# Where layer 1's first-norm modulation is computed: in layer 0's mixer, or at the end of layer 0's routing

## The chip, the cores and the metric

The kernel runs on one core of a Trainium2 chip. The metric is the device time of one execution, in microseconds (us), as the median over several executions. Within a core, PE is TensorE (matmuls; PEld its weight loads), DVE VectorE, ACT ScalarE, POOL GpSimd and SP SyncE, whose queue issues most DMAs here. Each engine works through its own instructions in order and waits on semaphores for the others.

## The reference

Two layers; each has an adaLN-modulated mixer and an adaLN-modulated mixture of experts. Cut to what bears on the change (c and c_ctx are vectors of 1024; x and ctx have 256 tokens each):

```python
for l in range(DEPTH):                                   # DEPTH = 2
    mod  = silu(c) @ w_mod[l] + b_mod[l]                 # 1024 x 6144
    sh1, sc1, g1, sh2, sc2, g2 = split(mod, 6)
    modc = silu(c_ctx) @ w_mod[l] + b_mod[l]             # the same for the context
    h_l = rmsnorm(xl, norm1_g[l]) * (1 + sc1) + sh1
    h_c = rmsnorm(xc, norm1_g[l]) * (1 + sc1c) + sh1c
    o_l, o_c = mixer(h_l, h_c, ...)                      # attention + SSD, w_out
    xl, xc = xl + g1 * o_l, xc + g1c * o_c
    y = hier_moe(h2 of all tokens, ...)                  # 4 groups x 8 experts, top 2
    xl, xc = xl + g2 * y_l, xc + g2c * y_c
return rmsnorm(xl, final_g)
```

The change concerns `sh1, sc1` and their context twins of layer 1. They depend on `c`, `c_ctx` and weights alone, so they can be computed at any time before layer 1's mixer.

## The kernel before

The kernel goes through layer 0's mixer (0 to some 258 us), its routing (output projection, second norm, router, to some 342 us), a branch for token counts over an expert's capacity, layer 0's experts (352 to some 615 us), and then the same for layer 1.

The two products `sh1, sc1` of layer 1 are 1024 x 2048 weights, cut into eight blocks of 1 MB. `mod_norm1(l)` (L203 ff.) is a generator that handles one block at a time: load the block into a tile of the pool `wh` ("wl"), eight matmuls that leave 32 x 256 partial sums each in four column groups (L221; a float32 matmul counts twice in the trace, so a block is 16 instructions there), a copy of the sums from PSUM to SBUF on DVE (`mr`, L223), two small matmuls that add the four groups and turn the result over (L227, four instructions in the trace), and three small DVE operations that make one column of `b1` (shift) and `a1` (norm gain times 1 + scale) of them (L228 to L230). A list `MODS` puts the modulations of a layer into one chain, and a planner weaves that chain with attention and SSD by estimated costs. In before, `MODS[0]` has three entries, and the third, `(1, 0)`, is `mod_norm1(1)`: its eight blocks lie between 213 and 259 us, near the end of layer 0's attention.

Layer 0's routing ends in a stretch that is ordered by hand. After the last router matmuls (`rmat`, L1110), `pick` finds the experts of the tokens on DVE, with one matmul group (L1161); `place` gives each token its slot in an expert's list (PE L1168, L1169), `onehot` and `spread` (PE L1195) write these lists, a GpSimd gather then fetches the token rows, `count` (PE L1463, DVE L1465, L1466) makes the largest count of an expert, `cmi`. Every engine loads `cmi` and takes or passes over the branch of `fallback` (L1805). The branch's body is only run when an expert has more tokens than its capacity. Behind it stand the last three loads of layer 0's first experts (`LATE`), the turning of the gathered rows (L1584, then `xgT`, L1593 and L1595), and the first expert matmul (L1608).

The tiles of the first experts' weights come from a ring ("R"), the pool `big` ("B", ten tiles of 1 MB) and the pool `wh` ("W"), in the order of the string `LOAD_TAGS[0]`; some come in quarters into small tiles (L256). Their DMAs are issued by SP, in order. `big` is the only pool of the three that the change also uses.

Of the kernel before, what the change touches and what calls it, by code (L numbers as in the profile page):

```python
# [4 lines left out]
F32 = mybir.dt.float32  # L5
# [15 lines left out]
BIG_BUFS = 10  # L21
LOOK = 3
BIG = 1.0e30
LOAD_TAGS = ("RBBBBBBBBWWWWBB", "RBBBBBBWWWWBBBB")
RAW = ("RRRBRRR", "RBBRRRR")
H2M = "AVAV"
H2A = "GGGGVVVV"
# [28 lines left out]
TAIL_ENG = {ET.PE, ET.DVE, ET.Activation, ET.Pool}  # L56
FIN_ENG = {ET.PE, ET.DVE, ET.Activation, ET.Pool}
ME = {ET.PE}
MODS = (((0, 1), (0, 2), (1, 0)), ((1, 1), (1, 2)))
ATT_W = (70.0, 45.0)  # L60
SSD_W = (28.0, 15.0)
MOD_W = (28.0, 18.0)
# [18 lines left out]
def _tile_kernel(tc, A, out, dbg=None):  # L81
# [15 lines left out]
    def bk():  # L97
        return psB.tile([128, 512], F32, tag="bk", name="bk")
# [13 lines left out]
    def big(name, dt=F32):  # L112
        return P.tile([128, 2048], dt, tag="big", name=name, bufs=BIG_BUFS)
# [13 lines left out]
    def sm(shape, tag, bufs=1, dt=F32):  # L127
        return P.tile(shape, dt, tag=tag, name=tag, bufs=bufs)
# [46 lines left out]
    def kcs(n):  # L175
        o, w = KC[n]
        return kd[:, o - KC_A:o - KC_A + w] if o >= KC_A else kc[:, o:o + w]

    def cps(n, l):
        o, w = CPK[n]  # L180
        return cpk[:, o + l * (w // 2):o + (l + 1) * (w // 2)]
# [30 lines left out]
    def mod_norm1(l, pre=()):  # L212
        a1 = cp.tile([128, 2, 8], F32, tag="a1", name="a1", bufs=2)
        b1 = cp.tile([128, 2, 8], F32, tag="b1", name="b1", bufs=2)
        modT[l, "a1"], modT[l, "b1"] = a1, b1
        for b in range(8):
            w = pre[b] if b < len(pre) else rload(A["wm0"][l, b], [128, 8, 256], big("wm") if pre else None)
            pm = md_()
            for k in range(8):
                g = k % 4  # L220
                T.matmul(pm[32 * g:32 * g + 32, 0:256], csT[:, k, :], w[:, k], start=(k < 4), stop=(k >= 4))  # L221
            mr = tw("bm", 2, "mr")[:, 0:256]
            V.tensor_copy(mr, pm[:, 0:256])  # L223
            yield 0.9
            pt = tp()
            for s in range(2):
                T.matmul(pt[:, 2 * s:2 * s + 2], mr[:, s * 128:(s + 1) * 128], kcs("sel"), start=True, stop=True)  # L227
            V.tensor_scalar(b1[:, :, b], pt[:, 0:2], cps("bsh", l)[:, b:b + 1], None, op0=ALU.add)  # L228
            V.tensor_scalar(a1[:, :, b], pt[:, 2:4], cps("bsc", l)[:, b:b + 1], 1.0, op0=ALU.add, op1=ALU.add)
            V.tensor_scalar(a1[:, :, b], a1[:, :, b], cps("n1g", l)[:, b:b + 1], None, op0=ALU.mult)  # L230
            yield 0.1

    def qload(src, tags, after=None):
        q = []
# [760 lines left out]
    def route_out(l, oT):  # L995
# [12 lines left out]
        for hf in range(2):  # L1008
            for b in range(2):
                wo[b, hf] = rload(A["wout"][l, b, hf], [128, 4, 512], big("wo") if WOB[l][2 * hf + b] == "B" else wh("wo"))  # L1010
        R = {}
        R["lg"] = sm([128, 4, 36], "lg")
        R["m1"] = sm([128, 4, 1], "m1")
        R["v8"] = sm([128, 4, 8], "v8")
# [148 lines left out]
        def place(pair):  # L1163
            s2 = slice(pair[0], pair[0] + 2)
            M, pk = Mf[:, s2], pkf[:, s2]
            j = pair[0] - qt[0]
            pp = pos[:, 32 * j:32 * j + 64]
            T.matmul(pp, lt, M, start=(j == 0), stop=False)  # L1168
            T.matmul(pp[:, 32:64], ones, M[:, 0], start=False, stop=True)  # L1169
            for t in pair:  # L1170
                for k in range(2):
                    V.scalar_tensor_tensor(tk2[:, t, k], keyf[:, t], k8[:, t, k:k + 1], pp[:, 32 * (t - pair[0]):32 * (t - pair[0]) + 32],
                                           op0=ALU.is_equal, op1=ALU.mult)
            V.reduce_sum(pk, tk2[:, s2], axis=AX.X)
            if l:
                sd = sm([128, 2, 2], "sd")
                ob = sm([128, 2, 2], "ob")
                er = sm([128, 2, 2], "er")
                V.scalar_tensor_tensor(er, k8[:, s2, 0:2], 1.0, k8[:, s2, 0:2], op0=ALU.is_ge, op1=ALU.subtract)
                V.scalar_tensor_tensor(sd, er, 64.0 * cap, pk, op0=ALU.mult, op1=ALU.add)  # L1180
                V.tensor_scalar(ob, pk, float(cap), 1.0e6, op0=ALU.is_ge, op1=ALU.mult)
                V.tensor_tensor(sd, sd, ob, op=ALU.add)
                for i in range(2):
                    V.tensor_tensor(R["sid"][:, i], sd[:, i].unsqueeze(2).to_broadcast([128, 2, 8]),
                                    boff.unsqueeze(1).to_broadcast([128, 2, 8]), op=ALU.add)
                return
            for t in pair:
                onehot(t)
            spread(pair)
# [40 lines left out]
        def h2w(t):  # L1230
            (nc.sync if t < 2 else nc.scalar).dma_start(h2d[l][t * 128:(t + 1) * 128, :], hres[t])
            dump(f"h2_{l}_{t}", hres[t])
# [74 lines left out]
        with tc.manual_schedule(engines=TAIL_ENG):  # L1307
            for b in range(2):
                prod(7, 2, b, tail)
                mul(2, b, banks[b, 2])  # L1310
            add(2, 0, G)
            add(2, 1, G)
            if l == 0:
                h2p(2, 0)
            prod(6, 3, 0, held)
            prod(7, 3, 0, tail)
            mul(3, 0, banks[0, 3], ("p", 3))
            add(3, 0, V)
            prod(6, 3, 1, held)
            prod(7, 3, 1, tail)  # L1320
            mul(3, 1, banks[1, 3], ("p", 3))
            add(3, 1, V)
            turn(2, 0)
            turn(3, 0)
            sqr(2, 0)
            mean(2, 0, 0)
            keep(2, 0, S)
            sqr(3, 0)
            mean(3, 0, 0)
            turn(2, 1)  # L1330
            rmat(2, 0)
            turn(3, 1)
            keep(3, 0, V)
            rmat(3, 0)
            sqr(3, 1)
            mean(3, 1, 1)
            root(3)
            keep(2, 1, V)
            rmat(2, 1)
            sqr(2, 1)  # L1340
            mean(2, 1, 1)
            root(2)
            if l == 0:
                h2p(2, 1)
            keep(3, 1, V)
            rmat(3, 1)
            if l == 0:
                h2s(2, 0)
                h2s(2, 1)
                h2a(3, 0, V)  # L1350
                h2b(3, 0, G)
                h2a(3, 1, V)
                h2b(3, 1, G)
                h2w(3)
            pick(prev)
            if l == 0:
                h2b(2, 0, G if HB[0] == "G" else V)
                h2b(2, 1, G if HB[1] == "G" else V)
                h2w(2)
                for t in prev:  # L1360
                    tokens(t)
            place(prev)
# [27 lines left out]
    def moe(l, R):  # L1390
# [121 lines left out]
        if l == 0:  # L1512
            count()
            R["gates"]()
            S.activation(sm([128, 1], "warm"), mhalf[:, 0:1], AF.Silu)
            fallback(l, R, gt4, cmi)
            for i in LATE[l]:
                load(i, gate)
# [441 lines left out]
```

## Time and profile before

| | |
|---|---|
| median of 3 runs | 1053.13 us (1052.07 to 1054.06) |
| the profiled execution | 1051.03 us, span 1049.2 us |
| mean granted TensorE clock | 0.964 |
| busy share of the span | PE 89%, DVE 59%, POOL 34%, ACT 32% |
| moved by DMA | 306 MB, mean 292 GB/s |

The profiled execution is 2.1 us under the median of the runs, and its span 1.8 us under its own time. Times of the rows are microseconds from the span's start. A busy share is an average over stages: in layer 0's attention PE is busy nearly all the time, in layer 0's routing it is not, in layer 1's experts the DMA is.

### The profile page before, as it was taken

To read this page: it belongs to the slowest core of one execution; us is meant where nothing else is said; L and a number is where in the kernel's file an instruction comes from. 1 tells how busy PE (TensorE), PEld (TensorE's weight loads), DVE (VectorE), ACT (ScalarE), POOL (GpSimd) and SP (SyncE) were. 2 spreads that over 40 slices of the span, in tenths; PEclk is the share of its full clock that TensorE was granted. 3 is DMA by queue.
4 is the path that set the end of the run, shared out by engine and by line. 5 is a ranking of instruction groups with operands and counts; after the bars stand their busy time and mean duration, and the time that the engine had idled before them with its cause. 6 is when DMAs were issued, how large, how long until landed. Compare 5 with 4: busy or idle time off the path is not lost. (4 is left out here: it accounts for less than half of the span.)

```text
span 1049.2 us, 14473 instructions
## 1 busy us (share of the span) xinstructions
PE 937.4 (89%) x5244; PEld 547.5 (52%) x5244; DVE 621.3 (59%) x1351; ACT 333.8 (32%) x689; POOL 356.2 (34%) x366
## 2 busy tenths in 40 slices
PE   5999999999987699999999979999999798786776
PEld 3778745566766344444444428683678543332232
DVE  4587079886688246666666667847886543222123
ACT  4465344544452110111112136543464211110102
POOL 2130035320175247667676560003331021111013
PEclk9999999999997799999999999999999898989989
DMA  9612377786748879899999835647486899998994
GB/s 375 208 43 79 141 302 248 281 309 221 294 126 295 288 306 404 335 418 419 419 419 420 341 111 171 239 163 261 173 315 248 281 417 419 419 419 353 421 414 159
DMA packets 54674, 306.20 MB, mean 292 GB/s; under 512 B 6168, under 2 KB 7064, under 8 KB 22976
## 3 DMA queue, kind: packets, MB, share of 16 engines
q1 hardware_dynamic: 49120, 288.10, 70.1%
q0 software_dynamic: 4224, 15.21, 4.6%
q10 hardware_dynamic: 1248, 1.86, 0.5%
q8 instruction: 44, 0.72, 0.3%
q14 instruction: 38, 0.31, 0.1%
HBM read 300.89 MB, written 4.26 MB: 291 GB/s over the span
## 5 line engine op out<-in xcount | busy, mean ns | idle before, releaser
L1673 POOL TENSOR_TENSOR xs<-xs,tmp 128x512 f32<-128x512 f32 x144 | 180.3, 1289 | 182.8 <-DVE tmp L1672 178.2
L1608 PE MATMUL bk<-we,xgT 128*64 128x512 f32 (+1 forms) x926 | 189.1, 615 | 14.6 <-DMA we<-wgu 14.6
L1643 PE MATMUL sc<-we,sa 128*64 128x512 f32 (+1 forms) x448 | 107.1, 645 | 17.5 <-DMA we<-wdn 17.5
L1608 PEld LDWEIGHTS bk<-we,xgT 128*64 128x64 f32 (+1 forms) x926 | 53.9, 126 | 124.0 <-issue 93.1
L1613 ACT ACTIVATE sa<-bk 128x256 f32<-128x256 f32 x24 | 9.2, 383 | 258.1 <-PE bk L1608 258.1
L1658 DVE SCALAR_TENSOR_TENSOR yl<-sc,gs,yh 128x512 fp32r<-128x512 f32 x46 | 34.4, 747 | 72.3 <-ACT yh L1657 72.3
L1643 PEld LDWEIGHTS sc<-we,sa 128*64 128x64 f32 (+1 forms) x448 | 28.2, 132 | 77.4 <-issue 43.5
L1657 ACT ACTIVATE yh<-sc,gs 128x512 fp32r<-128x512 f32 x46 | 31.6, 687 | 104.5 <-PE sc L1643 100.4
L1614 DVE TENSOR_TENSOR sa<-sa,bk 128x256 f32<-128x256 f32 x24 | 9.9, 412 | 71.6 <-ACT sa L1613 71.6
L770 PE MATMUL sc<-kT,qT 128*128 128x512 f32 (+1 forms) x96 | 45.7, 559 | 0.0
L792 PE MATMUL py<-pT,vt 128*64 128x128 f32 x320 | 43.6, 280 | 1.1 <-DVE oT L821 1.1
L1608 PE MATMUL bk<-ring,xgT 128*64 128x512 f32 (+1 forms) x80 | 40.5, 651 | 3.6 <-issue 2.5
L1072 DVE TENSOR_TENSOR lo<-wo,hi 128x512 fp32r<-128x512 f32 x44 | 33.8, 772 | 16.2 <-PE sc L1255 8.6
L1649 DVE TENSOR_SCALAR P<-kc,tid 128x128 fp32r<-128x128 f32 x80 | 40.8, 567 | 1.1 <-PE bk L1608 0.6
L792 PEld LDWEIGHTS py<-pT,vt 128*64 128x64 f32 x320 | 32.5, 136 | 15.4 <-issue 8.2
L774 ACT ACTIVATE p<-sc,mx 128x512 f32<-128x512 f32 (+1 forms) x48 | 29.4, 612 | 33.7 <-DVE mx L772 26.6
L401 PE MATMUL bk<-wh,hH 128*128 128x256 f32 (+1 forms) x128 | 39.8, 311 | 0.2
L1672 DVE TENSOR_TENSOR tmp<-bk,g 128x512 f32<-128x512 f32 x37 | 25.6, 691 | 23.9 <-POOL xs L1673 23.6
L403 PE MATMUL bk<-wh,hL 128*128 128x256 f32 (+1 forms) x128 | 38.0, 297 | 1.1 <-DVE hL L382 1.0
L785 ACT ACTIVATE pT<-tp 128x512 f32<-128x512 f32 (+1 forms) x48 | 24.9, 522 | 41.2 <-PE tp L783 41.1
L1582 PE MATMUL tp<-PT,h 128*128 128x128 f32 x256 | 34.3, 298 | 4.1 <-DVEq L1805 2.1
L1582 PEld LDWEIGHTS tp<-PT,h 128*128 128x128 f32 x256 | 32.8, 211 | 9.6 <-issue 5.4
(426 smaller groups left out, 2161.8 us busy)
## 6 DMA issues: line engine op xcount, KB each, us to landing
we<-wgu SPq DMA_DIRECT2D x109, 1024.0 KB, 17.7
we<-wdn SPq DMA_DIRECT2D x55, 1024.0 KB, 15.8
wl<-wmod SPq DMA_DIRECT2D x22, 1024.0 KB, 5.0
wl<-wm SPq DMA_DIRECT2D x10, 1024.0 KB, 8.1
ring<-wgu SPq DMA_DIRECT2D x10, 1024.0 KB, 19.8
wo<-wout SPq DMA_DIRECT2D x8, 1024.0 KB, 5.8
we<-wgu SPq DMA_DIRECT2D x27, 256.0 KB, 5.1
wm<-wm SPq DMA_DIRECT2D x6, 1024.0 KB, 12.2
```

Of the source, the lines that this page charges most:

```text
L401: T.matmul(o, a[0], b[0], start=start, stop=False)
L403: T.matmul(o, a[1], b[0], start=False, stop=stop)
L770: T.matmul(pm[:, 0:nk], qT[:, e, t * 128:(t + 1) * 128], kT[:, e, 0:nk], start=True, stop=True)
L792: T.matmul(py[e * 64:(e + 1) * 64, 0:128], vts[0][:, k, h * 64:(h + 1) * 64], pT[:, k * 128:(k + 1) * 128], start=(k == 0), stop=(k == nk ...
L1072: eng.tensor_tensor(lo, src, hi.bitcast(F32), op=ALU.subtract)
L1582: T.matmul(p_, R["hres"][t][:, c], xg[j], start=(j == 0), stop=(j == nT - 1))
L1608: T.matmul(pg[c], xgT[b][part][:, k, c], w[i][k], start=(part == 0 and k == 0), stop=(part == 1 and k == 3))
L1643: T.matmul(pd[h][c], aT[:, k, c], w[i][2 * k + h], start=(k == 0), stop=(k == 1))
L1649: V.tensor_scalar(Pm[b][:, j * 128:(j + 1) * 128], iota, tid[:, j, b:b + 1], None, op0=ALU.is_equal)
L1657: S.activation(yh, pd[h], AF.Copy, scale=gs[:, b:b + 1])
L1658: V.scalar_tensor_tensor(yl, pd[h], gs[:, b:b + 1], yh.bitcast(F32), op0=ALU.mult, op1=ALU.subtract)
L1673: (eng or (V if EADD[l][n] == "V" or alt and n % 2 else G)).tensor_tensor(xs[:, t, hs_], xs[:, t, hs_], tmp, op=ALU.add)
```

## The change

`(1, 0)` leaves `MODS[0]`, so `mod_norm1(1)` is no longer woven with layer 0's attention. A new generator `mod_next(1)` does its work in the routing. It has four tiles of the pool `big` ("wm"); blocks 0 to 3 are fetched by SP at once, blocks 4 to 7 each into the tile of the block four before it, once that block's matmuls are issued. `rows(b)` is the eight matmuls (now L253) and a copy of the sums to SBUF on ACT (L257) in place of DVE. The two small matmuls (L266) write into the same PSUM bank (`bk`, two buffers) as the sums, and two ACT operations (L267, L268) in place of three on DVE make the columns of `b1` and `a1`; a term `off` for the latter is made once on POOL. The matmuls of a block come ahead of the small ones of the block before it.

The generator is stepped by hand: its fetches at the start of the routing, three steps ahead of `pick(prev)` (blocks 0 to 3), one in `place` for the last pair of token tiles (block 4), and the rest after `count()` and ahead of the branch. In `LOAD_TAGS[0]` the four "W" move four places ahead, and a setting halves the memory in which GpSimd's DMA descriptors are kept.

```diff
-LOAD_TAGS = ("RBBBBBBBBWWWWBB", "RBBBBBBWWWWBBBB")
+LOAD_TAGS = ("RBBBBWWWWBBBBBB", "RBBBBBBWWWWBBBB")
-MODS = (((0, 1), (0, 2), (1, 0)), ((1, 1), (1, 2)))
+MODS = (((0, 1), (0, 2)), ((1, 1), (1, 2)))
+    def mod_next(l):
+        a1 = cp.tile([128, 2, 8], F32, tag="a1", name="a1", bufs=2)
+        b1 = cp.tile([128, 2, 8], F32, tag="b1", name="b1", bufs=2)
+        modT[l, "a1"], modT[l, "b1"] = a1, b1
+        off = sm([128, 8], "off")
+        G.tensor_scalar(off, cps("bsc", l), 1.0, None, op0=ALU.add)
+        G.tensor_tensor(off, off, cps("n1g", l), op=ALU.mult)
+        tiles = [big("wm") for _ in range(4)]
+
+        def fetch(b):
+            nc.sync.dma_start(tiles[b % 4], A["wm0"][l, b])
+
+        for b in range(4):
+            fetch(b)
+        yield
+        def rows(b):
+            w = tiles[b % 4].rearrange("p (k c) -> p k c", k=8)
+            pm = bk()
+            for k in range(8):
+                g = k % 4
+                T.matmul(pm[32 * g:32 * g + 32, 0:256], csT[:, k, :], w[:, k], start=(k < 4), stop=(k >= 4))
+            if b < 4:
+                fetch(b + 4)
+            mr = sm([128, 256], "mr", 2)
+            S.activation(mr, pm[:, 0:256], AF.Copy)
+            return pm, mr
+
+        cur = rows(0)
+        for b in range(8):
+            pm, mr = cur
+            if b < 7:
+                cur = rows(b + 1)
+            for s in range(2):
+                T.matmul(pm[:, 256 + 2 * s:258 + 2 * s], mr[:, s * 128:(s + 1) * 128], kcs("sel"), start=True, stop=True)
+            S.activation(b1[:, :, b], pm[:, 256:258], AF.Identity, bias=cps("bsh", l)[:, b:b + 1])
+            S.activation(a1[:, :, b], pm[:, 258:260], AF.Identity, bias=off[:, b:b + 1], scale=cps("n1g", l)[:, b:b + 1])
+            yield
@@ start of the routing
-        R = {}
+        nxt = mod_next(1) if l == 0 else iter(())
+        take(nxt, 1)
+        R = {"next": nxt}
@@ place
+            if pair[0] == 2:
+                take(nxt, 1)
             for t in pair:
                 onehot(t)
             spread(pair)
@@ the end of the routing
                 h2w(3)
+            take(nxt, 3)
             pick(prev)
@@ ahead of the branch
             count()
             R["gates"]()
+            drain(R["next"])
             S.activation(sm([128, 1], "warm"), mhalf[:, 0:1], AF.Silu)
             fallback(l, R, gt4, cmi)
@@
-    nc = bacc.Bacc("TRN2", target_bir_lowering=False, num_devices=1)
+    nc = bacc.Bacc("TRN2", target_bir_lowering=False, num_devices=1, dynamic_dma_scratch_size=8192)
```

Lines above the new function keep their numbers; below it a line of before stands 38 to 44 lines further down in the changed kernel.

On PE, in layer 0's attention, this stands in before (L770 scores, L783 turning of the probabilities, L792 values, L753 and L760 projections, L221 and L227 the modulation):

```order
L221 MATMUL md<-wl,kc 32x256 x8
L770 MATMUL sc<-kT,qT 128x512
L783 MATMUL tp<-kc,p 128x128 x4
L792 MATMUL py<-pT,vt 64x128 x4
L753 MATMUL bk<-kvqa,wl 128x512
L760 MATMUL bk<-kvqa,wl 128x512 x2
L227 MATMUL tp<-kc,mr 128x2 x2
L221 MATMUL md<-wl,kc 32x256 x5
L760 MATMUL bk<-kvqa,wl 128x512 x2
L221 MATMUL md<-wl,kc 32x256 x3
```

and this in the changed kernel (the same steps are L808, L821, L830, L791 and L798; L1078 is a small product for the router):

```order
L808 MATMUL sc<-kT,qT 128x512
L821 MATMUL tp<-kc,p 128x128 x4
L830 MATMUL py<-pT,vt 64x128 x2
L798 MATMUL bk<-kvqa,wl 128x512 x2
L1078 MATMUL md<-ke,sh_1490 128x36 x4
L798 MATMUL bk<-kvqa,wl 128x512 x2
```

The blocks are gone from between the attention's steps, and nothing has taken their place.

On PE, from the end of the router to the branch, before has `pick` (L1161), `place` (L1168, L1169), `spread` (L1195), `count` (L1463) and the branch:

```order
L1161 MATMUL md<-ke 128x64 x2
L1168 MATMUL md<-ke,kd 128x64
L1169 MATMUL md<-ke 128x32
L1195 MATMUL md<-rv,oh 128x32 x4
L1463 MATMUL md<-ke 128x32 x4
L1804 TENSOR_LOAD cmi
L1805 COMPARE_AND_BRANCH
```

The changed kernel has there first the blocks 0 to 3 and then the same steps with block 4 among them (L1201 is `pick`, L1208 and L1209 `place`, L1237 `spread`):

```order
L253 MATMUL bk<-wm,kc 32x256 x16
L266 MATMUL bk<-kc,mr 128x2 x2
L253 MATMUL bk<-wm,kc 32x256 x8
L266 MATMUL bk<-kc,mr 128x2 x2
L253 MATMUL bk<-wm,kc 32x256 x8
L266 MATMUL bk<-kc,mr 128x2 x2
L1201 MATMUL md<-ke 128x64 x2
L1208 MATMUL md<-ke,kd 128x64
L1209 MATMUL md<-ke 128x32
L253 MATMUL bk<-wm,kc 32x256 x8
L266 MATMUL bk<-kc,mr 128x2 x2
L1237 MATMUL md<-rv,oh 128x32 x4
```

and behind them `count` (L1506) and the blocks 5 to 7, up to the branch:

```order
L266 MATMUL bk<-kc,mr 128x2 x2
L253 MATMUL bk<-wm,kc 32x256
L1506 MATMUL md<-ke 128x32 x4
L253 MATMUL bk<-wm,kc 32x256 x7
L266 MATMUL bk<-kc,mr 128x2 x2
L253 MATMUL bk<-wm,kc 32x256 x8
L266 MATMUL bk<-kc,mr 128x2 x2
L253 MATMUL bk<-wm,kc 32x256 x8
L266 MATMUL bk<-kc,mr 128x2 x2
L1848 TENSOR_LOAD cmi
L1849 COMPARE_AND_BRANCH
```

All eight blocks now stand ahead of the branch, five of them ahead of `spread` and three between `count` and the branch.

On ACT, in the same stretch, before has two DMA issues and the two exponentials of the gates, and then the branch. The changed kernel has these, with the copies (L257) and the columns (L267, L268) around them (L1417 is the exponential that was L1374):

```order
L1273 DMA h2d_2251<-h_2911 128x1024
L257 ACTIVATE mr<-bk 128x256 x2
L267 ACTIVATE b_2261<-bk,kd 128x2
L268 ACTIVATE a_2260<-bk,off,kd 128x2
L1416 ACTIVATE e_3037<-e_3037 128x16
L1417 ACTIVATE gt<-dv 128x4
L257 ACTIVATE mr<-bk 128x256
L267 ACTIVATE b_2261<-bk,kd 128x2
L268 ACTIVATE a_2260<-bk,off,kd 128x2
L257 ACTIVATE mr<-bk 128x256
L267 ACTIVATE b_2261<-bk,kd 128x2
L268 ACTIVATE a_2260<-bk,off,kd 128x2
```

The copy of block 2 and all behind it now stand behind L1417, which waits for DVE's `dv`.

## Rows read from the trace of the kernel before

**Rows 1.** The page's part 1, busy time and share of the span:

```profile
PE 937.4 (89%) x5244; PEld 547.5 (52%) x5244; DVE 621.3 (59%) x1351; ACT 333.8 (32%) x689; POOL 356.2 (34%) x366
```

**Rows 2.** Windows; columns: length, busy PE, PEld, DVE, ACT, POOL, clock, DMA share, GB/s:

```profile
200.00:225.00 25.00, 25.00 (x163) 14.29 (x165) 21.17 (x55) 10.52 (x28) 7.42 (x9) 1.00 0.80 296
225.00:250.00 25.00, 24.58 (x198) 16.87 (x186) 19.32 (x59) 11.91 (x34) 7.60 (x8) 1.00 0.78 292
```

**Rows 3.** Lines by form, 125 to 300 us: the modulation's matmuls:

```profile
L221 PE MATMUL md<-wl,kc 128*32 128x256 f32 x128 | 10.6, 387 | 0.0
```

**Rows 4.** PE's timeline around one block in the weave (start, duration, line):

```profile
213.38 1.07 PE L221 MATMUL md<-wl,kc 128*32 128x256 f32 x16
214.38 1.12 PE L770 MATMUL sc<-kT,qT 128*128 128x512 f32 x2
...
219.13 0.50 PE L227 MATMUL tp<-kc,mr 128*128 128x2 f32 x4
219.57 1.05 PE L221 MATMUL md<-wl,kc 128*32 128x256 f32 x10
```

**Rows 5.** PE's timeline at the kernel's start, where layer 0's own blocks stand:

```profile
11.70 1.94 PE L221 MATMUL md<-wl,kc 128*32 128x256 f32 x16 [11.70 <-DVE xn L425]
13.57 1.12 PE L435 MATMUL py<-kc,xn 128*128 128x128 f32 x4
14.48 0.85 PE L227 MATMUL tp<-kc,mr 128*128 128x2 f32 x4
15.19 1.09 PE L435 MATMUL tp<-kc,xn 128*128 128x128 f32 x4
...
24.44 0.48 PE L402 MATMUL sc<-wl,hH 128*128 128x432 f32 x1
24.76 0.36 PE L403 MATMUL sc<-wh,hL 128*128 128x432 f32 x1
```

**Rows 6.** Windows around the end of the routing; columns as in rows 2:

```profile
318.00:328.50 10.50, 10.28 (x69) 8.85 (x68) 8.12 (x12) 4.10 (x10) 7.63 (x10) 1.00 0.91 317
329.00:339.40 10.40, 3.36 (x14) 2.90 (x13) 9.35 (x40) 1.14 (x3) 3.79 (x4) 0.50 0.84 315
...
353.00:363.00 10.00, 10.00 (x48) 4.18 (x44) 3.13 (x18) 0.00 (x0) 1.52 (x2) 0.86 1.01 380
```

**Rows 7.** PE's timeline from the router's end to the first expert matmul:

```profile
328.37 1.01 PE L1161 MATMUL md<-ke 128*128 128x64 f32 x4
334.49 0.69 PE L1168 MATMUL md<-ke,kd 128*128 128x64 f32 x2 [5.12 <-DVE ke L1156]
334.98 0.58 PE L1169 MATMUL md<-ke 128*128 128x32 f32 x2
337.21 1.92 PE L1195 MATMUL md<-rv,oh 128*128 128x32 f32 x8 [1.66 <-DVE oh L1125]
339.58 1.92 PE L1463 MATMUL md<-ke 128*128 128x32 f32 x8 [0.45 <-DVE idx L1487]
348.19 1.94 PE L1584 MATMUL tp<-kc,xg 128*128 128x128 f32 x8 [6.70 <-DVE we L138]
352.61 1.09 PE L1608 MATMUL bk<-ring,xgT 128*64 128x512 f32 x1 [2.48 <-issue]
```

**Rows 8.** DVE's timeline in the same stretch: the count, and the turned rows:

```profile
341.85 0.14 DVE L1466 CAST cmi<-cmx 128x1 int32<-128x1 f32 x1
...
351.83 0.68 DVE L1595 COPY xgT<-tp 128x512 f32<-128x512 f32 x1
```

**Rows 9.** ACT: its timeline at the gates, and the operations of one line:

```profile
334.08 0.21 ACT L1374 ACTIVATE gt<-dv 128x4 f32<-128x4 f32 x1 [1.88 <-DVE dv L1372]
...
L1613 ACT ACTIVATE sa<-bk x24: 383/383/384, 363.4 to 1018.6; 128x256 f32<-128x256 f32 x24
```

**Rows 10.** Waits, 340 or 353 to 620 us: total, times, longest:

```profile
PEld bk L1608 <- DMA we<-wgu: 0.3, 1, 0.3
...
SPq L139 <- PE bk L1608: 131.5, 25, 12.2
```

## The prediction

> **What bounds the kernel now.** I read the page's first part, then the windows of the two stretches that the change touches, then PE's timeline in both. PE is busy 89% of the span [rows 1], but that is an average, and the two stretches are opposite cases. In layer 0's attention PE is the bound: 25.00 and 24.58 us busy of 25 in two windows, at clock 1.00, with the DMA at 0.80 and 0.78 [rows 2]. What leaves PE's queue there shortens the stretch. At the end of the routing PE is busy 3.36 us of 10.40, at clock 0.50 [rows 6], because it waits for DVE's small operations: 5.12 us for `ke`, 1.66 for the one-hots, 0.45 for the gather's indices, and then 6.70 us around the branch [rows 7]. Work put into the first three of these holes could be free; work put between `count` and the branch is not, since PE has to take the branch itself.
>
> In the chain from the routing to the experts, `cmi` is ready at 341.99 [rows 8], PE is through `count` at 341.50, stands 6.70 us around the branch, turns the gathered rows (348.19 to 350.13), DVE copies them (351.83 to 352.51), and the first expert matmul starts at 352.61 [rows 7, 8]. From there on PE works without waiting for weights: one wait of 0.3 us for a load up to 620 us, while SP's queue waits 131.5 us for PE to release tiles [rows 10]. So a later start of the experts is not made up, and an earlier one is kept.
>
> **What the change gives.** Eight blocks leave the attention. In a place where PE has no gap, a block's matmuls occupy 1.00 us (213.38 to 214.38) and the small ones 0.44 (219.13 to 219.57) [rows 4]; there are eight, as the 128 instructions say [rows 3]. At most 8 x 1.44 = 11.5 us. PE is not quite saturated there (24.58 of 25), and without the blocks more of its waits will be bare, so I take 10.5; the lower bound is 7, if a third of what they fill turns into waits for DVE and ACT. The three DVE operations and the copy per block leave DVE too, which was 21.17 us busy of 25 [rows 2], so the bound is not likely to be reached.
>
> **What it costs at half clock.** The same work returns in the routing, and its price depends on the clock. In before the granted clock is 1.00 to 328.5 and 0.50 behind it [rows 6]: it fell although PE had been busy 10.28 us of 10.50, with transposes and 36-column products. At the kernel's start the same blocks take 1.87 us (11.70 to 13.57) and the small ones 0.71 (14.48 to 15.19); there they stood with transposes back to back, and PE was not brought to full clock by them: the 432-column matmul falls from 0.48 to 0.36 us only at 24.76, after a run of its like [rows 5]. The mix behind the router is the same, so I take 0.50 for it: 8 x (1.87 + 0.71) = 20.6 us of PE.
>
> Worked along PE's order, with all times on the clock of before (the attention's gain is taken off at the end). An ACT copy takes 0.38 us by the nearest row (128 x 256, [rows 9]) and a column operation some 0.2; with the passing on, I take 0.6 from a block's end to its `mr`, and 0.6 from the small matmuls to the second column.
> - Blocks 0 and 1: 328.4 to 332.15. Small matmuls of 0 to 332.9, their columns 333.5. Block 2 writes the bank of block 0, so it waits for these: 333.6 to 335.5. ACT's copy of block 2 stands behind the exponential that waits for DVE until 334.08 [rows 9]; that is over in time. Small ones of 1 to 336.2, their columns 336.9 (behind the copy of 2). Block 3: 337.0 to 338.9, small ones of 2 to 339.6.
> - Only now comes `pick`'s group (1.0) and `place` (1.07, from 334.49 to 335.56): 341.7 in place of 335.56, so 6.1 us late. DVE's `ke`, for which `place` waited in before until 334.49 [rows 7], now lies ready for 6 us; the one-hots follow 1.65 us behind, under block 4 (to 343.6) and the small ones of 3 (to 344.3).
> - `spread` (1.9) ends at 346.2 in place of 339.13. What is late next is the gather's indices, 7.1 us. Small ones of 4, `count` (1.9): 348.9. `cmi` would be ready 7.4 us late.
> - The rest stands bare ahead of the branch: the remainder of block 5 (1.7), then each time a copy (0.6), small ones (0.71) and the next block (1.87), up to the small ones of block 7 at 358.4. That is 16.4 us behind the 342.0 at which PE loaded `cmi` in before.
> - The branch costs what it did: `cmi` 341.99 to 348.19, 6.2 us [rows 7, 8], so 364.6; turning and copying, which no longer wait for the late loads on SP, 1.94 and some 0.8: 367.3, against 352.61.
>
> The experts of layer 0 start 14.7 us later, less 10.5: **+4.2 us**. On one side stands a branch whose stall has partly passed by then (2 us less), on the other side the lower gain of the attention (3.5 more): +2 to +8. The profiled execution was 1051.03 and the median of the runs 2.1 above; on the median's basis 1053.13 + 4.2 = 1057.3.
>
> [...]
>
> **What I cost at nothing.** The 8 MB are only moved. The routing's windows have the DMA at 0.84 [rows 6], the stretch that loses the blocks had 0.80 [rows 2], and the experts' first weights are wanted 14.7 us later behind the router than before; the cover is SP's 131.5 us of waiting for tiles [rows 10]. If it were gone, 8 MB at the 380 GB/s of rows 6 are 22 us, some of which would show as PE waits for loads; I take that for less than 1 in 10. The refetches of blocks 4 to 7 stand on SP behind PE's blocks 0 to 3, and behind them SP's remaining quarters and loads: block 4 is asked for at 330.3 and wanted at 341.7. POOL's two operations find it idle (3.79 us busy of 10.40, [rows 6]); that and the halved descriptor memory I leave at 0.
>
> **The rivals.**
> *The clock stays full (faster).* If PE keeps 1.00 behind the router, or is lifted within the first blocks, the same walk goes with 1.00 and 0.44: blocks 0 and 1 to 330.4; block 2 to 332.6; now ACT's order binds, its copy of block 2 waits until 334.3, block 3 is done at 336.3, `place` at 337.8 (2.2 late), `spread` at 340.5 (1.3 late), `count` at 342.2 (0.7 late), and the last small ones at 348.3, that is 6.3 late. Turning takes half as long, so that the experts start some 4 us late, less 10.5: -6.5, 1046.6 us. For it: the blocks make PE much denser than the 3.36 us of 10.40 in before, and at 213 us they run at full clock. Against it: the fall came while PE was dense, and rows 5. It decides from the point at which the clock is up by block 3.
> [...]
> *The clock comes back half-way (no change).* If it is up behind `spread`, the blocks 5 to 7 and the turning run at full clock and with 0.6 us of copy between them they cost 3 x 1.14 + 1 = 4.4 us less: +4.2 - 4.4 = 0, 1053 us. Later blocks stand closer together than the first four, which speaks for it; each waits for a copy, which speaks against.
> *The attention gives nothing much back (slower still).* If the woven blocks only filled waits for DVE, the gain would be 5 and the time 1063. PE's 25.00 of 25 [rows 2] are against it.
> *The loads come late (slower still):* as above, up to some 1065.
>
> **How the numbers follow.** A measurement of this kernel can tell about 0.2%, 2.1 us, from no change. Half clock, as worked: 0.54; half clock with less gain or late loads: 0.08; the clock back half-way, or the bounds meeting: 0.11; full clock: 0.27. The likeliest gives 1057.3 us, with a range of its own of 1055 to 1061. The full-clock case has too much weight to leave out, so the range for 8 in 10 runs from 1046 to 1061.5; outside it lie a full clock with the whole 11.5 us of gain, and the two slow rivals. Slower 0.61 (the half-clock case less its low edge), same 0.12, faster 0.27.
>
> **What would show it.** In the profile of the changed kernel: no L221 from 200 us on, and a start of the output projection some 10.5 us earlier (7 would be the lower bound). The blocks behind the router, 1.9 us for 16 instructions if the clock is low and 1.0 if not, and the granted clock of that window. `place` some 6 us further behind the router's last product than before, PE's load of `cmi` 30 us behind it (before 13.5), and then 6 us around the branch. No PE waits for loads in layer 0's experts, and layer 1 unchanged, shifted only. I am wrong if the clock is 1.00 in that stretch, if the attention shortens by less than 7 us, or if PE's waits for weights return.

## The result, and the profile after

The changed kernel takes 1060.27 us against 1054.38 (medians of 20 runs each); the ratio is 1.0052, with a 95% interval from 1.0038 to 1.0066. That is 5.5 us slower (4.0 to 7.0). One execution of the changed kernel in the slow state (1071.92 us) is left out of the ratio. The forecast was 4.2 us slower, within a range that holds the result.

PE's timeline of the changed kernel from the last router product to the first expert matmul (start, duration, line, and in brackets the idle time ahead and what ended it), which answers to [rows 7]:

```profile
318.54 1.06 PE L1150 MATMUL py<-rwp,xT 128*128 128x36 f32 x8
319.53 3.49 PE L253 MATMUL bk<-wm,kc 128*32 128x256 f32 x32
323.51 0.61 PE L266 MATMUL bk<-kc,mr 128*128 128x2 f32 x4 [0.49 <-ACT mr L257]
324.72 1.07 PE L253 MATMUL bk<-wm,kc 128*32 128x256 f32 x16 [0.60 <-ACT a L268]
...
326.92 1.94 PE L253 MATMUL bk<-wm,kc 128*32 128x256 f32 x16 [0.60 <-ACT a L268]
...
330.55 0.63 PE L1208 MATMUL md<-ke,kd 128*128 128x64 f32 x2
...
334.23 1.89 PE L1237 MATMUL md<-rv,oh 128*128 128x32 f32 x8
...
337.85 1.92 PE L1506 MATMUL md<-ke 128*128 128x32 f32 x8
339.70 1.93 PE L253 MATMUL bk<-wm,kc 128*32 128x256 f32 x14
342.18 1.01 PE L266 MATMUL bk<-kc,mr 128*128 128x2 f32 x4 [0.55 <-issue]
...
349.06 1.01 PE L266 MATMUL bk<-kc,mr 128*128 128x2 f32 x4 [0.56 <-ACT mr L257]
356.33 1.94 PE L1628 MATMUL tp<-kc,xg 128*128 128x128 f32 x8 [6.26 <-PEq L1849]
359.05 1.09 PE L1652 MATMUL bk<-ring,xgT 128*64 128x512 f32 x1 [0.78 <-DVE xgT L1639]
```

The 5.12 us in which PE waited ahead of `place` in [rows 7] are filled with blocks, and more: `place` (L1208) now follows blocks 0 to 3 without a wait. Between `count` (L1506) and the branch PE works on blocks 5 to 7, in which each small pair waits 0.55 us for the copy. The same stretch in windows (length, busy PE, PEld, DVE, ACT, POOL, clock, DMA share, GB/s), for [rows 6]:

```profile
318.00:323.00 5.00, 5.00 (x47) 2.92 (x46) 4.47 (x10) 1.44 (x2) 5.00 (x5) 0.67 0.52 154
323.00:326.50 3.50, 2.24 (x26) 1.46 (x24) 3.50 (x17) 1.99 (x8) 0.88 (x1) 0.98 0.92 320
326.50:351.00 24.50, 21.47 (x128) 13.85 (x128) 5.49 (x30) 5.34 (x19) 3.40 (x4) 0.50 1.00 383
```

The clock fell, came back for 3.5 us, and was at 0.50 for the remaining 24.5 us, although PE was busy 21.47 of them. The DMA, at 0.60 to 0.84 there in before, is saturated at 1.00. DVE's timeline at the end of the stretch, the copies that hold the late loads back and the copy of the turned rows (answers to [rows 8]):

```profile
358.10 0.21 DVE L138 COPY we<-gate 128x1 f32<-128x1 f32 x2 [9.33 <-SPq L1849]
358.23 0.68 DVE L1639 COPY xgT<-tp 128x512 f32<-128x512 f32 x1
```

DVE waited until 358.10 for SP (SPq L1849 is SP at the end of the branch, where it waited for its loads to land, one after the other, four waits of 15.1 us in all: the load issued at 339.40 landed 10.1 us later, at 349.5, and SP went on to the next wait at 349.6), and PE's turning ended at 356.33 + 1.94 = 358.27. Two waits with different causes ended together.

To compare kernels by stage, five starts on PE were read in each trace: the last instruction of the router's products (R), the start of the turning (T), the first expert matmul (M), the last product of layer 0's experts (E), the last one of the kernel (F), us:

| kernel | R | T | M | E | F | M-R | E-M | F-E |
|---|---|---|---|---|---|---|---|---|
| before | 328.3 | 348.2 | 352.6 | 619.6 | 1041.3 | 24.3 | 267.0 | 421.7 |
| before again | 330.3 | 350.9 | 355.1 | 622.1 | 1044.2 | 24.8 | 267.0 | 422.1 |
| after | 319.3 | 356.3 | 359.1 | 627.2 | 1052.8 | 39.8 | 268.1 | 425.6 |
| after again | 319.5 | 354.2 | 357.9 | 626.0 | 1049.3 | 38.4 | 268.1 | 423.3 |
| no blocks | 316.5 | 337.2 | 339.1 | 605.3 | 1026.7 | 22.6 | 266.2 | 421.4 |
| fill | 317.6 | 354.9 | 362.0 | 628.8 | 1049.5 | 44.4 | 266.8 | 420.7 |
| settings | 331.4 | 350.6 | 352.6 | 619.2 | 1044.0 | 21.2 | 266.6 | 424.8 |
| two in the hole | 326.8 | 346.5 | 348.4 | 615.4 | 1037.9 | 21.6 | 267.0 | 422.5 |
| descriptor memory | 330.8 | 349.9 | 354.9 | 621.8 | 1043.9 | 24.1 | 266.9 | 422.1 |
| old tiles | 319.1 | 353.6 | 355.6 | 622.2 | | 36.5 | 266.6 | |
| loads only | 320.8 | 351.1 | 362.0 | 630.4 | 1053.0 | 41.2 | 268.4 | 422.6 |
| late loads | 319.4 | 351.0 | 353.0 | 620.1 | 1041.6 | 33.6 | 267.1 | 421.5 |
| three in the experts | 318.8 | 346.9 | 348.8 | 622.3 | 1045.7 | 30.0 | 273.5 | 423.4 |
| tiles and late loads | 330.1 | 349.6 | 351.5 | 618.5 | 1040.6 | 21.4 | 267.0 | 422.1 |

Single traces differ by chance: F-E lies between 420.7 and 425.6 without any change in layer 1, and R by 2 us between the two traces of before. M-R is the steady measure of the tail. By the second pair the account is 10.8 us won up to R, 13.6 lost from R to M, 1.1 in layer 0's experts, 1.2 in layer 1: 5.1 us, close to the 5.5 of the medians. By the first pair 9.0 are won and 15.5 lost.

### The profile page after: what moved, and what is told of

Read it like the earlier page. It is cut to its first block, busy times and chain, and to the rows that moved or that the text cites. A ratio compares the mean times of both kernels' runs of the same rounds, so it can differ in the third digit from the quotient of the medians.

```text
span 1061.2 us, 14482 instructions
## 1 busy us (share of the span) xinstructions
PE 946.9 (89%) x5244; PEld 550.8 (52%) x5244; DVE 613.9 (58%) x1319; ACT 340.1 (32%) x713; POOL 356.4 (34%) x368
## 5 line engine op out<-in xcount | busy, mean ns | idle before, releaser
L1652 PE MATMUL bk<-we,xgT 128*64 128x512 f32 (+1 forms) x926 | 188.1, 606 | 15.5 <-DMA we<-wgu 15.5
L808 PE MATMUL sc<-kT,qT 128*128 128x512 f32 (+1 forms) x96 | 46.5, 569 | 0.3 <-ACT p L812 0.3
L830 PE MATMUL py<-pT,vt 128*64 128x128 f32 x320 | 44.4, 283 | 0.0
L830 PEld LDWEIGHTS py<-pT,vt 128*64 128x64 f32 x320 | 33.1, 138 | 16.8 <-issue 8.4
L439 PE MATMUL bk<-hH,wh 128*128 128x512 f32 (+1 forms) x96 | 37.7, 393 | 0.0
```

Source lines behind the costliest of these rows:

```text
L439: T.matmul(o, a[0], b[0], start=start, stop=False)
L808: T.matmul(pm[:, 0:nk], qT[:, e, t * 128:(t + 1) * 128], kT[:, e, 0:nk], start=True, stop=True)
L830: T.matmul(py[e * 64:(e + 1) * 64, 0:128], vts[0][:, k, h * 64:(h + 1) * 64], pT[:, k * 128:(k + 1) * 128], start=(k == 0), stop=(k == nk ...
L1652: T.matmul(pg[c], xgT[b][part][:, k, c], w[i][k], start=(part == 0 and k == 0), stop=(part == 1 and k == 3))
```

## The experiments

All ratios are against the kernel before in the same series, with 95% intervals.

**No blocks.** The body of `mod_next` is two constants:

```diff
-        tiles = [big("wm") for _ in range(4)]
...
+        G.memset(a1, 1.0)
+        G.memset(b1, 0.0)
+        yield
```

> The changed kernel with the eight blocks left out altogether (their loads too; layer 1's first shift and scale are constants, which is no longer the reference's computation). It prices what the attention gives back. Theory (the attention gains some 9 to 10.5 us, the tail costs 15): 1044 to 1046 us, 9 to 10 under the kernel before, with the end of the router's products some 9 us earlier and the way from there to the first expert matmul as long as before, 25 us. Rival (the blocks filled waits, so the attention gains 5 or less): 1049 us or more.

1037.42 us, ratio 0.9854 (0.9825 to 0.9884): 15.4 us less, more than either theory said. R is 11.8 us earlier than in before, so the attention gives back all that the blocks took (8 x 1.44 = 11.5). Most of the rest is in the tail: M-R is 22.6, some 2 us shorter, though the blocks were never there. So something else in the change is worth a few us.

**Settings.** The kernel before with the two settings:

```diff
-LOAD_TAGS = ("RBBBBBBBBWWWWBB", "RBBBBBBWWWWBBBB")
+LOAD_TAGS = ("RBBBBWWWWBBBBBB", "RBBBBBBWWWWBBBB")
-    nc = bacc.Bacc("TRN2", target_bir_lowering=False, num_devices=1)
+    nc = bacc.Bacc("TRN2", target_bir_lowering=False, num_devices=1, dynamic_dma_scratch_size=8192)
```

> The kernel before with the two settings of the change alone: the new order of the first weight tiles and the halved descriptor memory. Theory: no change, within 2 us of the kernel before. Rival (a part of the 5.5 us comes from the loads' order or from descriptors): slower by 2 us or more.

1049.21 us, ratio 0.9955 (0.9940 to 0.9971): the settings alone are worth 4.7 us. The theory fell. PE's timeline of this run:

```profile
342.69 1.92 PE L1463 MATMUL md<-ke 128*128 128x32 f32 x8 [0.45 <-DVE idx L1487]
350.65 1.94 PE L1584 MATMUL tp<-kc,xg 128*128 128x128 f32 x8 [6.04 <-DVEq L1805]
352.57 1.08 PE L1608 MATMUL bk<-ring,xgT 128*64 128x512 f32 x1
```

The first expert matmul follows the turning without the 2.48 us of [rows 7]. In before SP had issued a late 1 MB load (`we<-wdn`) at 342.91, ahead of the branch; DVE's copy of the turned rows (351.83) stood behind a copy that waited for SP, and SP for that load:

```profile
342.91 0.33 SPq L139 DMA_DIRECT2D we<-wdn  x1
351.72 1.03 SPq L139 DMA_DIRECT2D we<-wgu  x2
351.76 0.15 DVE L138 COPY we<-gate 128x1 f32<-128x1 f32 x1 [3.58 <-SPq L1805]
```

With the new order that load is issued behind the branch (350.82), and PE does not wait for its landing. M-R is 21.2 to 21.6 in the three kernels that have the new order and the blocks or most of them in the attention, and 24.1 to 24.8 in the three with the old order.

**Descriptor memory.** The second of the two settings alone.

> The kernel before with the halved descriptor memory alone. The two settings together made it 4.7 us faster, against the expectation. Theory (the order of the weight tiles does it: the load that stood ahead of the branch now stands behind it, so nothing waits for its landing): the halved memory changes nothing, within 2 us of the kernel before. Rival (descriptors do it): 3 us or more faster.

1055.75 us, ratio 1.0006 (0.9987 to 1.0025), M-R 24.1 as in before. No effect shows; the interval leaves room for 1.4 us less to 2.6 more.

**Tiles and late loads.** The first of the two settings alone, and `LATE` for layer 0 with six loads in place of three:

```diff
-LATE = ((15, 16, 17), (16,))
+LATE = ((13, 14, 15, 16, 17, 18), (16,))
```

> The kernel before, blocks in the attention, with the new order of tiles alone and the three last loads behind the branch. The two settings gave 4.7 us, the descriptor memory none of it. Theory (the gain is that nothing on SP lies ahead of the branch that is still to land; one late load was enough for that): as with the settings, 1048 to 1051 us, with SP's wait at the branch over ahead of PE. Rival (the settings' gain was something else, in the descriptors together with the tiles): 1053 or more.

1050.82 us, ratio 0.9979 (0.9958 to 0.9999); M-R is 21.4, as with the settings. The time agrees with the theory, though the interval against before is wide. **Before again** has the wait of [rows 7] once more, 2.32 us, on DVE's copy behind SP:

> The kernel before once more, for its trace. Theory: DVE waits again for SP at the branch, until the load that was issued ahead of it has landed, and the first expert matmul starts some 2.5 us behind the turning. Rival: that wait is chance, and the start follows the turning directly.

```profile
354.28 0.15 DVE L138 COPY we<-gate 128x1 f32<-128x1 f32 x1 [3.20 <-SPq L1805]
354.36 0.68 DVE L1595 COPY xgT<-tp 128x512 f32<-128x512 f32 x1
```

It is no chance, then: from T to M are 4.2 to 5.0 us in the three traces with the old order, 1.9 to 2.0 in the three with the new.

**Fill.** Behind each block's sums two matmuls without use (rows of `wm` by the identity), meant to keep the clock up:

```diff
+            fill = sc()
+            for n in range(2):
+                T.matmul(fill, ident, tiles[b % 4][:, n * 512:(n + 1) * 512], start=True, stop=True)
             if b < 4:
                 fetch(b + 4)
```

> The changed kernel with two idle 512-column matmuls behind each block's sums, which only keep PE's array streaming. Theory (the blocks cost much because PE's clock is at half there): the granted clock stays at 1.00 from the router to the branch, the stretch from the router's last product to the first expert matmul falls from 40 to some 32 to 35 us, and the time to 1053 to 1056. Rival (the cost is the chain of waits between PE, ACT and PE, whatever the clock): the fill comes on top, 1060 to 1064 us.

1061.35 us, ratio 1.0085 (1.0050 to 1.0119), in the rival's range. The clock did what the theory asks, the time did not. Windows of this run:

```profile
317.00:323.70 6.70, 6.70 (x29) 2.79 (x32) 5.75 (x21) 1.90 (x5) 4.80 (x4) 0.50 0.55 208
323.70:354.00 30.30, 26.27 (x196) 14.52 (x188) 6.21 (x32) 7.97 (x24) 3.40 (x4) 1.00 0.89 315
```

PE's timeline and DVE's:

```profile
341.53 1.07 PE L253 MATMUL bk<-wm,kc 128*32 128x256 f32 x16
342.53 1.13 PE L256 MATMUL sc<-wm,kc 128*128 128x512 f32 x2
343.49 0.50 PE L269 MATMUL bk<-kc,mr 128*128 128x2 f32 x4
343.86 1.10 PE L256 MATMUL sc<-wm,kc 128*128 128x512 f32 x2
...
350.22 0.95 PE L269 MATMUL bk<-kc,mr 128*128 128x2 f32 x8
354.90 1.94 PE L1631 MATMUL tp<-kc,xg 128*128 128x128 f32 x8 [3.74 <-DMA xg<-h2d,idx]
362.01 1.09 PE L1655 MATMUL bk<-ring,xgT 128*64 128x512 f32 x1 [5.17 <-DVE xgT L1642]
```

```profile
361.05 0.21 DVE L138 COPY we<-gate 128x1 f32<-128x1 f32 x2 [10.43 <-SPq L1852]
361.18 0.68 DVE L1642 COPY xgT<-tp 128x512 f32<-128x512 f32 x1
```

At full clock a block takes 1.00 us and the small pair 0.37 (starts at 341.53, 342.53; 343.49, 343.86), against 1.87 and 0.88 in the changed kernel (326.92, 328.79, 329.67). But the fill takes PE's time too: the last block's work ends at 351.17, 33.6 us behind R, where the changed kernel needs 30.8. And the rows' gather had not landed when PE came to it, and then DVE stood 10.4 us for SP's loads. PE's clock is not the only bound. The fill also delays the refetches (SP is through with them at 334.78, 17.2 us behind R, against 329.25, 10.0 behind, in the changed kernel), so the run doesn't separate the two; the next two do.

**Old tiles.** The lines `if b < 4: fetch(b + 4)` are left out.

> The changed kernel without the second four loads: blocks 4 to 7 are worked out from the tiles of blocks 0 to 3, which is not the reference's computation. PE's, ACT's and DVE's work is the same, 4 MB fewer are loaded in the tail. In the changed kernel two things end together at the branch, PE's queue (rows turned at 358.3) and SP's wait for its loads (357.9). Theory (either of them alone sets the start, so taking one away gives little): 1058 to 1061 us, SP's wait ends at least 3 us ahead of PE. Rival (the tail's price is that of the loads): 1055 or less.

Its total, 2842.34 us, says nothing on the change: with these values more tokens crowd into one expert of layer 1 than it has places, and the branch's body runs there. Layer 0 can be read: M-R is 36.5, 2 to 3 us shorter than in the changed kernel, SP issued its next load at 345.75, so its wait was over 8 us ahead of the turning, and PE's work ahead of the branch, with the branch itself, sets the start. So PE's work, with the first four loads only, costs 36.5 - 22.6 = 13.9 us.

**Loads only.** The loop over the blocks ends at 4; all eight are loaded.

```diff
-        for b in range(8):
+        for b in range(4):
             pm, mr = cur
-            if b < 7:
+            if b < 3:
```

> The other half: the changed kernel with all loads, but blocks 4 to 7 not worked out (their shift and scale are constants, not the reference's). PE reaches the branch some 12 us earlier. Theory (SP's wait for its loads is a second bound that ends at the same time): the first expert matmul moves by 3 us at most, because it waits for SP, and the time is 1056 to 1060. Rival (PE's blocks alone are the price, as predicted): 1047 to 1050, 11 us under the changed kernel.

1061.40 us, ratio 1.0072 (1.0045 to 1.0098): as slow as the changed kernel with half of PE's blocks gone, and 1.4 us above the theory's range. PE's timeline and DVE's of this run:

```profile
338.36 1.92 PE L1508 MATMUL md<-ke 128*128 128x32 f32 x8 [0.45 <-DVE idx L1532]
351.06 1.94 PE L1630 MATMUL tp<-kc,xg 128*128 128x128 f32 x8 [10.78 <-DMA xg<-h2d,idx]
361.98 1.09 PE L1654 MATMUL bk<-ring,xgT 128*64 128x512 f32 x1 [8.98 <-issue]
```

```profile
361.06 0.22 DVE L138 COPY we<-gate 128x1 f32<-128x1 f32 x2 [17.88 <-SPq L1851]
```

PE is through at 340.3 and then stands 10.8 us for the gather and 9.0 us for the copy behind SP. The loads, with four blocks on PE, cost 41.2 - 22.6 = 18.6 us here. The theory's bound held: the first expert matmul came no earlier at all, 41.2 us behind R.

**Late loads.** `LATE` with six loads, as in the diff above, in the changed kernel.

> The changed kernel with the three 1 MB loads that stand right ahead of the branch on SP put behind it, so that SP waits for less there; nothing else differs. Theory (PE's queue and SP's wait end together): SP's wait ends some 5 us earlier, the start stays where PE puts it, 1058 to 1061 us. Rival (SP's wait alone sets the start): 1056 or less.

1056.69 us, ratio 1.0019 (0.9990 to 1.0048), some 3.5 us under the changed kernel, though the two intervals overlap, and between the two theories. PE's timeline:

```profile
346.80 1.01 PE L266 MATMUL bk<-kc,mr 128*128 128x2 f32 x4 [0.56 <-ACT mr L257]
351.05 1.94 PE L1628 MATMUL tp<-kc,xg 128*128 128x128 f32 x8 [3.24 <-DVE we L138]
353.01 1.08 PE L1652 MATMUL bk<-ring,xgT 128*64 128x512 f32 x1
```

SP issued its next load at 349.22, so its wait was over ahead of the turning, and the start was PE's own. Against the changed kernel once more (M-R 38.4), whose PE was at the same point at 346.92, the start is 4.9 us sooner: 1.8 because nothing waits behind the turning, and 3.1 because PE turned the rows sooner, with 3.24 us idle around the branch in place of 6.21.

**After again**, to see whether these 3 us are chance:

> The changed kernel once more, for its trace: how much of the differences between single traces is chance. Theory: PE's branch takes 6 us again and SP's wait ends within 2 us of the turning of the rows; the falls of the clock lie elsewhere. Rival: the branch takes 3 us, as in the run with the late loads, so that it differs from execution to execution.

```profile
346.92 1.02 PE L266 MATMUL bk<-kc,mr 128*128 128x2 f32 x4 [0.57 <-ACT mr L257]
354.15 1.94 PE L1628 MATMUL tp<-kc,xg 128*128 128x128 f32 x8 [6.21 <-PEq L1849]
357.87 1.08 PE L1652 MATMUL bk<-ring,xgT 128*64 128x512 f32 x1 [1.78 <-DVE xgT L1639]
```

1059.49 us in a single run. The branch took 6.21 us again (6.26 in the first trace), so its length goes with the program rather than with chance. Here PE came 2.2 us sooner than in the first trace, and SP's wait (356.9) was the later of the two: of the two bounds now one, now the other ends last.

**Two in the hole.** Blocks 0 and 1 ahead of `pick`, 2 to 7 in the attention, with the settings of the change:

```diff
+MODS = (((0, 1), (0, 2), (1, 0)), ((1, 1), (1, 2)))
-        for b in range(8):
+        for b in range(first, 8):
...
-        tiles = [big("wm") for _ in range(4)]
+        tiles = [big("wm") for _ in range(2)]
```

> Blocks 0 and 1 as in the changed kernel, ahead of the choice of experts, blocks 2 to 7 in the attention as before. PE waits there 5.1 us for DVE, and two blocks take 2 x 2.58 = 5.2 us at half clock, fewer at full. Theory (what fits into that hole is free): the attention gains 2 x 1.3 us or so, the tail loses 0.5 at most, so 1 to 3 us under the kernel before, 1051.5 to 1053.5. Rival (the blocks in front of the choice delay it in any case): 1055 or more.

1050.26 us, ratio 0.9968 (0.9946 to 0.9990). The number lies under the theory's, but the settings alone gave 1049.21, so the two blocks gave nothing that shows. M-R is 21.6, not longer than without them (21.2, 21.4): in the hole they are free, as the theory has it. The other half is open. R lies at 326.8, and at 328.3 to 331.4 in the five traces with all blocks in the attention, so the 2.6 us for two blocks fewer may be there; the two medians do not show them, and single runs of either kernel spread over 6.6 to 8.4 us.

**Three in the experts.** Late loads, and blocks 5 to 7 between the matmuls of layer 0's first two expert batches:

```diff
-            drain(R["next"])
+            take(R["next"], 1)
...
                 stage_c(b + 1, 0)
+                if b < 2 and l == 0:
+                    take(R["next"], 1)
                 stage_c(b + 1, 1)
+                if b < 2 and l == 0:
+                    take(R["next"], 1)
...
```

> As the run with the late loads (1056.7 us), and blocks 5 to 7 taken from ahead of the branch into the first two batches of layer 0's experts, between their matmuls. Theory (ahead of the branch a block costs its matmuls at half clock and the copy that PE waits for, 3.4 us by the trace of the changed kernel; among the experts 1.44 us at full clock, since PE is the bound there): 3 x 2 = 6 us less, 1049 to 1053 us, with the branch reached some 10 us earlier and the experts some 4 us longer. Rival (the branch or the gathers then set the start, so that little comes earlier): 1055 to 1060.

1059.02 us, ratio 1.0053 (1.0026 to 1.0079), in the rival's range; the theory's 1049 to 1053 was missed. PE's timeline:

```profile
336.29 1.89 PE L1509 MATMUL md<-ke 128*128 128x32 f32 x8
346.90 1.94 PE L1631 MATMUL tp<-kc,xg 128*128 128x128 f32 x8 [8.72 <-DVE we L138]
...
364.21 1.07 PE L253 MATMUL md<-wm,kc 128*32 128x256 f32 x16
365.21 3.65 PE L1655 MATMUL bk<-we,xgT 128*64 128x512 f32 x16
...
376.74 0.50 PE L1715 MATMUL md<-yh,P 128*128 128x512 f32 x1 [0.60 <-ACT a L271]
```

PE was at the branch 9.6 us sooner (338.2 against 347.8), but stood 8.72 us around it, so the experts start only 4.2 us sooner than with late loads alone (348.8 against 353.0). The experts then took 6.4 us longer (273.5 against 267.1): three blocks at some 1.5 us, one wait of 0.60 for ACT, and 1.5 us in which PE waited for DVE's `tmp` ahead of one group of L1655. What PE gained ahead of the branch was lost around it and in the experts.

**The branch in the traces.** What PE does in these microseconds stands in the traces. The branch is one instruction of PE's sequencer (COMPARE_BRANCH, L1849 in the changed kernel), and it takes most of the time that PE stands idle: 6.37 us in the changed kernel, 3.33 with late loads, 7.35 with three blocks in the experts.

In 13 of the 14 traces it ends 1.3 to 1.5 us behind the end of one 16 KB packet on a DMA queue that the profile names "instruction" (q8). From the records of the packets, with the DMA's busy share between the branch's start and the packet's:

| kernel | branch starts | packet starts | packet ends | branch ends | DMA share |
|---|---|---|---|---|---|
| before | 342.62 | 345.35 | 346.51 | 347.88 | 0.84 |
| after | 349.65 | 353.55 | 354.71 | 356.02 | 1.02 |
| after again | 347.51 | 351.17 | 352.27 | 353.77 | 1.03 |
| old tiles | 346.60 | 350.86 | 351.94 | 353.32 | 0.82 |
| late loads | 347.40 | 348.41 | 349.37 | 350.73 | 0.02 |
| three in the experts | 339.23 | 344.18 | 345.24 | 346.58 | 0.96 |

With loads only the last such packet had ended 10 us ahead of the branch, and the branch took 0.35 us; with fill the packet started 0.7 us ahead of the branch. In the other twelve it started behind the branch. That PE stands in the branch for this packet is the author's estimate from these times. What differs between the traces is how soon the packet starts: 1.0 us behind the branch where late loads left the DMA idle, 1.7 to 5.0 in the eleven traces in which other transfers kept it busy (shares of 0.76 to 1.03). That these transfers delay it was not tested by itself, and the share alone does not order the traces. With three blocks in the experts a shorter branch would have gained little: the first gather of the rows, issued at 337.87, landed 8.9 us later, at 346.8, and the turning started at 346.90.

## Why the prediction was right, and where it was right for less than it said

**Direction and size.** Forecast 10.5 us won and 14.7 lost; by the two pairs of traces 9.0 to 10.8 won and 13.6 to 15.5 lost. Both terms hold. R is a mean of 330.2 in the five traces with all blocks in the attention and 318.9 in the eight with none there: 11.3 us, close to the upper bound of 11.5.

**The walk through the tail.** `place` was to be 6.1 us late; measured from R it starts at 330.55 - 319.3 = 11.2 in place of 334.49 - 328.3 = 6.2, 5.0 late. `cmi` was to be 7.4 late; `count` starts at 18.5 in place of 11.3, 7.2 late. PE was to leave the last block 30 us behind the router: 350.07 - 319.3 = 30.8. A small pair took 0.87 to 0.94 us where 0.71 had been taken from the kernel's start. The branch was put at 6.2 us and took 6.3 idle, partly by luck: in before the 6.2 hold a branch of 5.3 us and the way from `cmi` to it, here the branch alone is 6.4, and it was between 3.3 and 7.3 in programs close to this one. The first expert matmul was to be 14.7 us later and was 15.5 by the first pair, 13.6 by the second. One reading was off without effect: up to 620 us PE's weight loads wait twice for a load, 0.3 us each, and not once.

**The clock.** Half clock was right for the stretch from 326.5 on and for most of blocks 0 and 1 (3.49 us for 32 instructions); block 2 alone ran at full clock (1.07). The waits for ACT stood where the walk had them (0.49 and twice 0.60). In the run with fill, with 512-column matmuls between the blocks, the granted clock was 1.00 for 30.3 us, PE being busy 26.27 of them (87%). In the changed kernel, without them, it was 0.50, although PE was busy 21.47 us of 24.50 (88%).

**The step that was wrong at little cost.** "The 8 MB are only moved" was costed at nothing, on the ground that SP waits for tiles during the experts. That cover is real among the experts, but not at the branch: there SP waited for the loads that it had issued ahead of it (15.1 us in the changed kernel, with DVE behind it until 358.1), and with the refetched blocks the DMA is saturated from 326.5 to 351 (share 1.00). The runs with loads only (M-R 41.2) and with old tiles (36.5) show that loads and PE each set a start near that of the changed kernel; halving one leaves the other. The walk charged the turned rows with no wait for SP at all. That the total came out right owes something to luck: in the first trace the two bounds ended within 0.2 us of each other, in the second SP's was later and cost 1.78.

**The rival of the full clock** was given 0.27 and 1046.6 us. The clock was not full, and whether the time would have followed it is not shown: the fill lengthened PE's own work. Loads only speaks against it: PE was through with the count 19.4 us behind R there, and the first expert matmul still came 41.2 behind it. In the changed kernel's own trace DVE was held until 358.10, so a faster PE alone could have gained 0.2 us at that point. Whether a full clock would have brought the refetches forward too, which stand behind PE's blocks 0 to 3, no run tells. The wait of the loads was not priced in this rival.

**The settings** were costed as part of the branch's end (turning and copying at 2.7 us in place of 4.4, so 1.7 us, that "no longer wait for the late loads on SP"). Alone they are worth 4.7 us (3.1 to 6.3), about 3 of them seen in M-R; where the rest lies is open. If the two add, the change is a move that costs some 10 us (1.0052 over 0.9955), with a gain of nearly half that packed into it; the move without the settings was not run. The settings alone, 1049.21 us, beat both kernels.

**The experts' 1.1 us.** Layer 0's experts took 268.1 us in place of 267.0. The granted clock behind M was 0.50 for 5.1 us in the changed kernel (359.05 to 364.12) and for 3.2 in before (352.61 to 355.78); 1.9 us more at 0.50 are about 1 us of work, an estimate from a block's 1.87 us at 0.50 against 1.00 at 1.00.

**What stays open:** what decides how late the packet of the instruction queue (q8) starts behind PE's branch; whether two blocks fewer shorten the attention; and what a full clock would have made of the refetches.

## What to carry to other kernels

A hole in an engine's timeline is as large as the next thing that ends behind it: before work is moved into one, list everything that has to be over at the same point, the landing of loads too, and price each alone. Work that is moved takes its loads along; 8 MB that were hidden in one stage were here one of two bounds in another, where SP stood until its loads had landed (15.1 us in the changed kernel). Where a change carries settings with it, run them alone: here they were worth 4.7 us against a change of 5.5 the other way.

## What the runs showed of the hardware

PE's idle time between its last work ahead of a branch that is passed over and the turning behind it was 6.26 and 6.21 us in two executions of one program, 3.24 when three loads were moved behind the branch, and 8.72 when three blocks of work were moved behind it as well. Most of it was the branch instruction itself (6.37, 6.25, 3.33 and 7.35 us), which in 13 traces ended 1.3 to 1.5 us behind a 16 KB packet on the queue that the profile names "instruction" (q8), and took 0.35 us in the one trace without such a packet near it.

At the end of the branch SP waited, in the changed kernel, for the loads that it had issued ahead of it, from 342.5 to 357.9 us, with the last of them issued by 341.9.

The same matmuls (32 x 256 sums, 16 instructions) took 1.00 us at a granted clock of 1.00 and 1.87 at 0.50, and the clock was 0.50 throughout a stretch of 24.5 us in which PE was busy 21.47.
